# Projecting keys and queries before values in an attention block

## The chip, the cores and the metric

The kernel runs on one NeuronCore of a Trainium2 chip. The metric is the device time of one execution in microseconds, as the median of repeated runs. Five engines work side by side, each in its own order of instructions: PE (matrix products and transposes), DVE (VectorE), ACT (ScalarE), POOL (GpSimd) and SP, which here issues the loads and stores. They wait for each other by semaphores.

## The reference

One layer of a bidirectional encoder block on 512 tokens of 1024 values, all in float32:

```
h    = rms_norm(x) * (1 + scale1) + shift1
proj = h @ w_in        # columns: qa ka va | qb kb vb | gates
# branch A: 12 heads of 64, three groups with (window, dilation) =
#           (128, 1), (512, 4), (2048, 16), merged by their denominators
# branch B: 8 heads, differential attention:
#           (softmax(q1 k1) - lam * softmax(q2 k2)) v, then a sub-norm
# q and k of both branches: rms norm per head, then rotary embedding
mixed = sigmoid(gate_a) * (oa @ w_proj_a) + sigmoid(gate_b) * (ob @ w_proj_b)
x = x + gate1 * (mixed @ w_out)
x = x + gate2 * PEER(rms_norm(x) * (1 + scale2) + shift2)
```

The change lies in the part from `proj` to the two attention branches. The experts' part (PEER), which takes most of the span, comes after it.

## The kernel before

**A projection.** `proj` multiplies the normed input, held as eight transposed tiles, with a chunk of up to 512 columns of `w_in`. For each of the eight slices of the depth, `piece` loads 128 rows of the chunk (tile raw), and splits them into a high part (ScalarE, line 91, whi) and a low part (line 92, wlo, on VectorE or GpSimd); PE then issues three matmuls (lines 86 to 88) for each of four blocks of tokens. The four sums of a chunk fill four PSUM banks (`pmat`, tile pj, four buffers), which are freed when `done` has read them. A 512-column chunk is 96 matmuls.

**Three users of it.** `v_chunk` projects values, and ScalarE copies the sums to va (branch A) or vb (branch B) at line 479. `heads` projects keys or queries: ScalarE copies the sums to four tiles kraw at line 408 (there are eight kraw in all), and then come the head norms and the rotary embedding, on ScalarE (413), VectorE (414, a Newton iteration at 97 to 103, 426 to 428) and GpSimd (421, 429, the last step). `gate` adds a bias on VectorE (line 651) and applies a tanh.

**The units.** `pair_psum` (line 435) transposes the keys or queries of two heads out of the kraw tiles. `dil_units` goes through branch A in two pairs of head slots, eight units each: scores (lines 475, 476, 543, 544, on VectorE 546 to 553) and, two units later, an out (transposes at 561, ScalarE's copies at 563, the products with va at 568, VectorE's 570). `dif_units` goes through branch B in two halves of 16 units: scores at 475 and 476, VectorE 605 to 611, ScalarE 606, and an out (617, 619, products with vb at 623, 625).

**Their order.** The first chunks run alone (`run`). After that `merge` writes units (main) and projections (side) alternately: after each unit, as many slices of the side stream as its estimated cost times a ratio calls for. `seq` strings chunks one after the other, and `with_ada` adds parts of the modulation vectors' loads. The side streams are: beside the first dilated pair, the keys and queries of the second pair (384 columns each); beside the second pair, vb 0 and the keys and queries of the first half of branch B; beside the first half, vb 1 and the keys k1 and queries q1 of the second half (q1 goes to a tile of its own, not to kraw); beside the second half, three gate chunks and the projection of branch A. The fourth gate chunk, the projection of branch B and the rest follow.

**Who decides the order on an engine.** The program's order is a priority only. A list scheduler places the instructions of each engine at build time, by a timeline that it works out itself, as soon as it takes their inputs and buffers for ready. A tile of a rotating pool is had when its earlier user's last reader is done. The order on each engine is then fixed.

Of the kernel before, what the change touches and what calls it, by code (L numbers as in the profile page):

```python
# [45 lines left out]
def merge(main, side, ratio):  # L46

    a = b = 0.0
    live = True
    for c in main:  # L50
        a += c
        while live and b < a * ratio:
            try:
                b += next(side)
            except StopIteration:
                live = False
    if live:
        drain(side)
# [73 lines left out]
def front(K, A):  # L132
# [267 lines left out]
    def heads(c0, n, tab, jp=None, dst=None):  # L400

        H = n // 64
        raws = {}
        ss = wf.tile([128, 4, H], F32, name=f"ss{H}", bufs=2)

        def done(a, ps):
            raws[a] = dst[a] if dst else kq.tile([128, 512], F32, name="kraw", tag="kraw", bufs=8)[:, :n]
            nc.scalar.activation(raws[a], ps, AF.Copy)

        yield from proj(hT, win, c0, n, 8, done, jp)  # L410
        for a in range(4):
            sq = f2()
            nc.scalar.activation(sq[:, :n], raws[a], AF.Square)
            nc.vector.tensor_reduce(out=ss[:, a, :], in_=sq[:, :n].rearrange("p (h i) -> p h i", i=64), op=OP.add, axis=AX)
        v = wf.tile([128, 4 * H], F32, name=f"v{H}", bufs=2)
        nc.vector.tensor_scalar(v, ss.rearrange("p a h -> p (a h)"), 1.0 / 64, EPS, op0=OP.mult, op1=OP.add)
        r = wf.tile([128, 4, H], F32, name=f"r{H}", bufs=2)
        rsqrt(r.rearrange("p a h -> p (a h)"), v, 4 * H)
        for a in range(4):
            raw = raws[a].rearrange("p (h i) -> p h i", i=64)  # L420
            nc.gpsimd.tensor_tensor(raw, raw, r[:, a, :, None].to_broadcast([128, H, 64]), op=OP.mult)
            m2 = f2()
            m2v = m2[:, :n].rearrange("p (h i) -> p h i", i=64)
            C = ropeC[tab][:, a, None, :].to_broadcast([128, H, 64])
            S = ropeS[tab]
            nc.vector.tensor_tensor(m2v[:, :, 0:32], raw[:, :, 32:64], S[:, a, None, 0:32].to_broadcast([128, H, 32]), op=OP.mult)
            nc.vector.tensor_tensor(m2v[:, :, 32:64], raw[:, :, 0:32], S[:, a, None, 32:64].to_broadcast([128, H, 32]), op=OP.mult)
            nc.vector.tensor_tensor(raw, raw, C, op=OP.mult)
            nc.gpsimd.tensor_tensor(raws[a], raws[a], m2[:, :n], op=OP.add)
        return [raws[a] for a in range(4)]  # L430
# [47 lines left out]
    def v_chunk(c0, n, dst):  # L478
        return proj(hT, win, c0, n, 8, lambda a, ps: nc.scalar.activation(dst[:, a, :], ps, AF.Copy))

    def run(g):
        while True:
            try:
                next(g)
            except StopIteration as e:
                return e.value
# [24 lines left out]
    for i in range(2):  # L511
        q = []
# [6 lines left out]
    va = dil.tile([128, 4, 768], F32, name="va")  # L519
# [12 lines left out]
    def dil_keys(jp, ok):  # L532
        return k_pair(pair_psum(ok, 0)), k_raw(pair_psum(ok, 1)), k_raw(pair_psum(ok, 2))

    def dil_queries(oq):
        return q_pair(pair_psum(oq, 0)), q_raw(pair_psum(oq, 1), 0), q_raw(pair_psum(oq, 2), 1)
# [57 lines left out]
    vbs = [vp.tile([128, 4, 512], F32, name=f"vb{i}", tag=f"vb{i}") for i in range(2)]  # L594
# [61 lines left out]
    def seq(*gens):  # L656
        for g in gens:
            yield from g
# [6 lines left out]
    def with_ada(g, vecs=ada2):  # L665
        while True:
            try:
                c = next(g)
            except StopIteration as e:
                return e.value  # L670
            next(vecs, None)
            yield c

    run(v_chunk(1536, 512, va[:, :, 0:512]))
    run(v_chunk(2048, 256, va[:, :, 512:768]))
    ok = run(heads(768, 384, 0, 0))
    oq = run(heads(0, 384, 1, 0))
    late_ = cst.tile([128, 1], F32, name="later")
    nc.vector.tensor_copy(late_, oq[0][:, 0:1])
    mark[0] = late_  # L680
# [2 lines left out]
    def keep(name, g):  # L683
        res[name] = yield from g

    k, q = dil_keys(0, ok), dil_queries(oq)
    merge(pipelined(dil_units(0, k, q)),
          seq(keep('k', heads(768, 384, 0, 1)), keep('q', heads(0, 384, 1, 1))), 3.0)
    k, q = dil_keys(1, res['k']), dil_queries(res['q'])
    merge(pipelined(dil_units(1, k, q)),  # L690
          with_ada(seq(v_chunk(4352, 512, vbs[0]), keep('k', heads(3328, 512, 2)), keep('q', heads(2304, 512, 3)))), 3.0)
    dil.close()
    dif = Pool("dif")
    ob = dif.tile([128, 4, 1024], F32, name="ob")
# [2 lines left out]
    dx = Pool("dx")  # L697
    q1 = gen.tile([128, 4, 512], F32, name="q1", tag="Tl1")
    merge(pipelined(dif_units(0, res['k'], res['q'])),
          with_ada(seq(v_chunk(4864, 512, vbs[1]), keep('k1', heads(3840, 512, 2)),  # L700
                       keep('q1', heads(2816, 512, 3, dst=[q1[:, a, :] for a in range(4)])))), 1.5)
    oaT = ([], [])

    def oa_rows():
# [572 lines left out]
```

## Time and profile before

| | us |
|---|---|
| median of 3 runs | 2019.08 (2017.93 to 2024.71) |
| the profiled execution | 2023.89 |
| its span in the profile | 2022.1 |
| PE busy in the span | 1879.2 |
| DVE busy | 1629.3 |
| ACT busy | 842.7 |
| POOL busy | 819.5 |

Busy times of matmuls overlap and are modelled, so a busy PE is not a PE at its peak. Times in rows are microseconds from the start of the span. In brackets behind an instruction stands the idle time of its engine just before it, and who ended it.

### The profile page before, as it was taken

The numbers are of one execution on the slowest core, as the hardware profiler recorded it, in microseconds if no ns is written. First come the engines' busy times: TensorE is split into PE (matmuls) and PEld (weight loads), VectorE is DVE, ScalarE is ACT, GpSimd is POOL, SyncE is SP. The second block draws the span as 40 slices with busy tenths as digits, with TensorE's granted clock in tenths as the row PEclk, the third lists the DMA queues.
The fourth block names the chain that finished last, engine by engine and source line by source line (L and its number), as shares of the span: only waits on it lengthen the run. The fifth ranks groups of instructions, "written<-read, shape, count | busy, mean of one in ns | idle before, by whom it ended". The sixth has DMA issues, their size and how long they took to land.

```text
span 2022.1 us, 28380 instructions
## 1 busy us (share of the span) xinstructions
PE 1879.2 (93%) x9858; PEld 1623.4 (80%) x9858; DVE 1629.3 (81%) x3228; ACT 842.7 (42%) x1330; POOL 819.5 (41%) x582
## 2 busy tenths in 40 slices
PE   6999998989899899999999999979997999899898
PEld 5987777778677788999989999958885788679676
DVE  7489585886875759999989999579886887888778
ACT  3444454645633333345455566423332333233222
POOL 2554332352145531012533000465565454656445
PEclk9999998999999999999999999989998999899999
DMA  7334242132256322578779867889988988998888
GB/s 260 91 114 121 62 142 62 32 89 84 58 156 211 132 79 66 157 246 284 250 272 319 283 231 254 295 320 363 336 288 302 354 310 312 353 337 323 299 308 292
DMA packets 206418, 447.30 MB, mean 221 GB/s; under 512 B 17298, under 2 KB 104643, under 8 KB 206147
## 3 DMA queue, kind: packets, MB, share of 16 engines
q1 hardware_dynamic: 168592, 309.14, 45.3%
q0 software_dynamic: 36864, 134.23, 18.4%
q10 hardware_dynamic: 818, 2.12, 0.3%
q8 instruction: 77, 1.26, 0.3%
q14 instruction: 67, 0.54, 0.1%
HBM read 397.20 MB, written 48.23 MB: 220 GB/s over the span
## 4 chain that ended last, share of the span: by engine, by line
PE 38%; DVE 13%; issue 11%; DMA 9%; POOL 7%; ACT 1%; SPq 0%; POOLq 0%; DVEq 0%; ACTq 0%
PE y L1220 10%; PE pj L86 8%; PE pj L87 8%; PE pj L88 8%; POOL gat L1058 4%; POOL wlo L92 2%; PE pg L1137 2%; DMA gat<-expert_v,eidx 2%; DVE wlo L92 2%; DMA gat<-expert_u,eidx 2%; DMA am<-gls 2%; DMA raw<-uT 1%; DMA raw<-expert_v 1%; DMA raw<-w_ada 1%; DVE mr L933 1%
## 5 line engine op out<-in xcount | busy, mean ns | idle before, releaser
L91 ACT ACTIVATE whi<-raw 128x1024 fp32r<-128x1024 f32 (+3 forms) x431 | 382.2, 893 | 460.3 <-PE pj L88 116.8
L92 POOL TENSOR_TENSOR wlo<-raw,whi 128x1024 fp32r<-128x1024 f32 (+2 forms) x140 | 275.6, 1972 | 465.2 <-ACT whi L91 437.5
L92 DVE TENSOR_TENSOR wlo<-raw,whi 128x1024 fp32r<-128x1024 f32 (+3 forms) x291 | 326.4, 1126 | 100.0 <-ACT whi L91 99.2
L86 PE MATMUL pj<-h2h,whi 128*128 128x384 f32 x1008 | 345.7, 343 | 6.3 <-ACT am L879 6.3
L88 PE MATMUL pj<-h2h,wlo 128*128 128x384 f32 x1008 | 343.6, 341 | 7.3 <-DVE wlo L92 4.1
L87 PE MATMUL pj<-h2l,whi 128*128 128x384 f32 x1008 | 344.3, 342 | 0.0
L1058 POOL DMA_INDIRECT gat<-expert_u,eidx x128 | 174.3, 1362 | 325.9 <-DVE gscr L1064 152.7
L1220 PE MATMUL y<-wlo,ah 128*128 128x512 f32 x768 | 248.0, 405 | 44.2 <-POOL wlo L92 44.2
L1058 POOL DMA_INDIRECT gat<-expert_v,eidx x128 | 199.4, 1557 | 204.4 <-DVE acc L1076 127.8
L1220 PE MATMUL y<-whi,al 128*128 128x512 f32 x768 | 240.6, 402 | 0.0
L1220 PE MATMUL y<-whi,ah 128*128 128x512 f32 x768 | 229.7, 396 | 7.4 <-ACT ah L91 6.3
L1220 PEld LDWEIGHTS y<-wlo,ah 128*128 128x128 f32 x768 | 147.0, 193 | 83.7 <-POOL wlo L92 48.5
L86 PE MATMUL pj<-whi,hh 128*128 128x512 f32 (+2 forms) x512 | 192.5, 389 | 9.5 <-DVE gA L651 4.4
L91 ACT ACTIVATE ah<-am 128x384 fp32r<-128x384 f32 x128 | 67.0, 524 | 318.7 <-PE y L1220 217.4
L87 PE MATMUL pj<-wlo,hh 128*128 128x512 f32 (+2 forms) x512 | 196.7, 385 | 2.3 <-DVE wlo L92 2.3
L86 PEld LDWEIGHTS pj<-h2h,whi 128*128 128x128 f32 x1008 | 191.2, 190 | 9.0 <-ACT am L879 7.5
L88 PEld LDWEIGHTS pj<-h2h,wlo 128*128 128x128 f32 x1008 | 190.8, 189 | 8.8 <-DVE wlo L92 4.8
L87 PEld LDWEIGHTS pj<-h2l,whi 128*128 128x128 f32 x1008 | 190.9, 189 | 1.2
L88 PE MATMUL pj<-whi,hl 128*128 128x512 f32 (+2 forms) x512 | 191.5, 381 | 0.0
L1076 DVE SCALAR_TENSOR_TENSOR acc<-gat,wts,acc 128x1024 f32<-128x1024 f32 x127 | 182.0, 1433 | 11.5 <-DMA gat<-expert_v,eidx 10.8
L1220 PEld LDWEIGHTS y<-whi,ah 128*128 128x128 f32 x768 | 143.8, 188 | 42.3 <-ACT ah L91 8.1
L1220 PEld LDWEIGHTS y<-whi,al 128*128 128x128 f32 x768 | 147.7, 192 | 36.6 <-DVE al L92 0.2
(313 smaller groups left out, 3274.0 us busy)
## 6 DMA issues: line engine op xcount, KB each, us to landing
raw<-uT SPq DMA_DIRECT2D x128, 512.0 KB
raw<-expert_v SPq DMA_DIRECT2D x128, 512.0 KB
gd<-stage SPq DMA_DIRECT2D x48, 512.0 KB
gch<-gd SPq DMA_DIRECT2D x16, 1536.0 KB
raw<-w_in SPq DMA_DIRECT2D x88, 256.0 KB
am<-gls SPq DMA_DIRECT2D x96, 192.0 KB
gls<-am SPq DMA_DIRECT2D x94, 192.0 KB
raw<-w_ada SPq DMA_DIRECT2D x64, 256.0 KB
```

The lines of the kernel that those rows point to most:

```text
L86: nc.tensor.matmul(ps, lh, rh, start=start, stop=False)
L87: nc.tensor.matmul(ps, lh, rl, start=False, stop=False)
L88: nc.tensor.matmul(ps, ll, rh, start=False, stop=stop)
L91: nc.scalar.activation(hi, raw, AF.Copy)
L92: (eng or nc.vector).tensor_tensor(lo, raw, hi.bitcast(F32), op=OP.subtract)
L933: nc.vector.match_replace(out=r, in_to_replace=v[:, 0:8], in_values=s, imm_value=-3.0e38)
L1058: nc.gpsimd.indirect_dma_start(out=t, out_offset=None, in_=src, in_offset=bass.IndirectOffsetOnAxis(ap=eidx[:, s:s + 1], axis=0))
L1076: nc.vector.scalar_tensor_tensor(acc, t, wts[:, s:s + 1], acc, op0=OP.mult, op1=OP.add)
L1137: nc.tensor.matmul(p[:, j * 128:j * 128 + 128], oh[1][:, :, q + j], pcs[i][:, q + j, :], start=i == 0, stop=i == 1)
L1220: nc.tensor.matmul(ys[b][n], l[:, bs], r[:, n * 512:n * 512 + 512], start=n_ == 0 and i == 0, stop=n_ == 127 and i == 2)
```

## The change

Three chunks of values move behind the keys and queries that stand beside them. Nothing else is changed.

```
     run(v_chunk(1536, 512, va[:, :, 0:512]))
-    run(v_chunk(2048, 256, va[:, :, 512:768]))
     ok = run(heads(768, 384, 0, 0))
     oq = run(heads(0, 384, 1, 0))
+    run(v_chunk(2048, 256, va[:, :, 512:768]))
...
     merge(pipelined(dil_units(1, k, q)),
-          with_ada(seq(v_chunk(4352, 512, vbs[0]), keep('k', heads(3328, 512, 2)), keep('q', heads(2304, 512, 3)))), 3.0)
+          with_ada(seq(keep('k', heads(3328, 512, 2)), keep('q', heads(2304, 512, 3)), v_chunk(4352, 512, vbs[0]))), 3.0)
...
     merge(pipelined(dif_units(0, res['k'], res['q'])),
-          with_ada(seq(v_chunk(4864, 512, vbs[1]), keep('k1', heads(3840, 512, 2)),
-                       keep('q1', heads(2816, 512, 3, dst=[q1[:, a, :] for a in range(4)])))), 1.5)
+          with_ada(seq(keep('k1', heads(3840, 512, 2)),
+                       keep('q1', heads(2816, 512, 3, dst=[q1[:, a, :] for a in range(4)])),
+                       v_chunk(4864, 512, vbs[1]))), 1.5)
```

## Rows read from the trace of the kernel before

**Rows 1.** The page: busy time by engine, and the chain that ended last.

```profile
PE 1879.2 (93%) x9858; PEld 1623.4 (80%) x9858; DVE 1629.3 (81%) x3228; ACT 842.7 (42%) x1330; POOL 819.5 (41%) x582
...
PE 38%; DVE 13%; issue 11%; DMA 9%; POOL 7%; ACT 1%; SPq 0%; POOLq 0%; DVEq 0%; ACTq 0%
```

**Rows 2.** Timeline of ACT: the copies that end a projection (start, duration, instruction).

```profile
63.31 2.04 ACT L479 ACTIVATE va<-pj 128x512 f32<-128x512 f32 x4
...
74.22 1.31 ACT L479 ACTIVATE va<-pj 128x256 f32<-128x256 f32 x4
...
90.22 1.01 ACT L408 ACTIVATE kraw<-pj 128x384 f32<-128x384 f32 x2
...
106.86 1.01 ACT L408 ACTIVATE kraw<-pj 128x384 f32<-128x384 f32 x2
...
195.59 0.58 ACT L479 ACTIVATE vb<-pj 128x512 f32<-128x512 f32 x1
...
229.04 1.58 ACT L408 ACTIVATE kraw<-pj 128x512 f32<-128x512 f32 x3
...
369.86 1.57 ACT L408 ACTIVATE kraw<-pj 128x512 f32<-128x512 f32 x3
```

**Rows 3.** Timeline of PE: transposes of keys and queries; first and last matmul of gate chunks.

```profile
109.22 0.44 PE L435 MATMUL pt<-ident,kraw 128*128 128x128 f32 x2 [0.61 <-POOL kraw L429]
111.23 0.69 PE L435 MATMUL pt<-ident,kraw 128*128 128x128 f32 x2 [1.57 <-POOL kraw L429]
...
226.02 2.54 PE L435 MATMUL pt<-ident,kraw 128*128 128x128 f32 x16
...
368.73 0.60 PE L435 MATMUL pt<-ident,kraw 128*128 128x128 f32 x4
...
439.54 0.79 PE L86 MATMUL pj<-whi,hh 128*128 128x512 f32 x1 [4.42 <-DVE gA L651]
...
503.11 0.39 PE L88 MATMUL pj<-whi,hl 128*128 128x512 f32 x1
```

**Rows 4.** Timeline of POOL: the last rope step of the first queries.

```profile
131.71 1.55 POOL L429 TENSOR_TENSOR kraw<-kraw,f 128x384 f32<-128x384 f32 x1 [0.50 <-DVE g L183]
```

**Rows 5.** Windows: stretch, length, busy by engine (instructions), clock, DMA share, GB/s.

```profile
75.00:91.00 16.00, 16.00 (x94) 16.00 (x94) 2.28 (x4) 5.32 (x12) 4.22 (x7) 1.00 0.38 110
...
108.00:116.00 8.00, 5.82 (x28) 5.27 (x27) 7.65 (x21) 3.64 (x8) 4.95 (x4) 0.79 0.27 79
116.00:144.00 28.00, 25.22 (x141) 24.33 (x140) 22.86 (x45) 15.26 (x29) 16.23 (x16) 0.94 0.40 119
...
158.00:195.00 37.00, 34.87 (x186) 28.09 (x186) 35.72 (x76) 14.37 (x31) 18.72 (x16) 1.00 0.40 116
195.00:229.00 34.00, 32.55 (x180) 26.89 (x180) 10.12 (x18) 14.70 (x29) 6.14 (x5) 1.00 0.36 108
...
340.00:368.00 28.00, 21.81 (x121) 16.06 (x120) 24.69 (x50) 20.46 (x50) 2.31 (x3) 0.94 0.04 10
...
404.00:440.00 36.00, 29.24 (x149) 24.01 (x148) 33.93 (x63) 14.77 (x33) 21.89 (x16) 0.98 0.21 57
```

**Rows 6.** Windows for line 568 alone: PE, PEld, clock, DMA share, GB/s.

```profile
195.00:229.00 34.00, 6.25 (x48) 6.44 (x48) 1.00 0.36 108
```

**Rows 7.** Timeline of PE: two outs of dilated units with little projection between.

```profile
258.43 1.55 PE L568 MATMUL pt<-va,eT 128*128 128x64 f32 x12
...
262.37 1.00 PE L568 MATMUL pt<-va,eT 128*128 128x64 f32 x8
```

**Rows 8.** Windows for line 623 alone; a differential unit has eight records.

```profile
404.00:440.00 36.00, 4.21 (x32) 4.19 (x32) 0.98 0.21 57
...
456.00:503.00 47.00, 4.21 (x32) 4.18 (x32) 1.00 0.26 80
503.00:536.00 33.00, 11.32 (x80) 9.76 (x80) 1.00 0.16 47
```

## Prediction before the change was measured

> **What bounds the kernel now.** I read the page first. PE is busy for 93% of the span, yet its share of the chain that ended last is 38%, with 13% DVE and 11% in which nothing visible is waited for [rows 1]. So a busy PE is no proof of a bound, and the stretch that the edit touches has to be read by itself. I took it in four steps: ScalarE's copies that end each projection (they date the chunks), PE's timeline around the transposes that read keys and queries, GpSimd's last rope step, and last the busy times by stage.
>
> The copies give the order and the pace [rows 2]: the 256-column value chunk takes 74.22 − 63.31 = 10.9 us of PE, the first keys follow at 90.22, the first queries at 106.86, the first vb at 195.59, the next keys at 229.04, k1 at 369.86. Two different limits show by stage [rows 5]. From 116 to 195 us DVE is nearly full (22.86 of 28 us, 35.72 of 37): the rope of keys and queries and the score sums of the first dilated pair. From 195 to 229 it is the other way: PE 32.55 of 34 us, DVE 10.12. From 340 to 368 PE runs differential units alone (21.81 of 28).
>
> The third thing to see is a buffer. Keys and queries share eight kraw tiles, four per call of heads(). The key copies at 229.04 come right behind the sixteen transposes at 226.02 that free four of them, and the k1 copies at 369.86 right behind the transposes at 368.73 [rows 2, 3]. Until such a copy is made, its chunk holds all four pj banks and no other projection can start.
>
> **The change, part by part.** Nothing is removed or added. The same loads, splits, matmuls and copies are issued; three chunks of values move behind the keys and queries beside them, with the weight loads on SP's queue and their splits on ScalarE and DVE.
>
> First move: the 256-column chunk goes behind the first queries. Keys and queries come forward by its 10.9 us. The rope that follows is long: the queries' copies begin at 106.86 and GpSimd's last sum ends at 131.71 + 1.55 = 133.3 [rows 2, 4], 26 us, and the first scores wait for it. DVE can take that work earlier, since it is busy for only 2.28 of 16 us from 75 to 91 [rows 5]. In PE's order the moved chunk now lies where PE waits 0.61 and 1.57 us for the keys' rope [rows 3] at a granted clock of 0.79 [rows 5], so those 2.2 us of PE should go too. How far the first dilated units come forward isn't shown by any row: at least the 2.2 us of PE, at most 10.9. The bounds are far apart; DVE's 13.7 idle us from 75 to 91 decide for the upper end, and I take 10.
>
> Second move: the 512 columns of keys take the slot that vb 0 has, so their matmuls end at about 195.6 − 10 = 186 instead of just before 229. But their copies need the four kraw tiles that the second dilated pair's keys hold until their transposes, which stand behind all outs of the first pair. Behind the waiting copies are queued the four pj banks, so PE has no projection, and the queries, vb 0 and all later chunks wait. That is a new stall. What is left to do in it: four outs. With projections between them four outs took the 34 us from 195 to 229 (48 records of line 568, 12 to a unit [rows 6]), 8.5 us each, while DVE stood idle: they wait their turn in PE's order. With little projection about, two outs stood 262.37 − 258.43 = 3.9 us apart [rows 7]. So the stall is 4 × 3.9 = 16 us, the transposes and the first key copy take some 2.5 more, as now from 226.02 to 229.04, and the copies come at 186 + 16 + 2.5 = 204.5. Call the lead X = 229 − 204.5 = 24.5 us. Bounds: X is 2 if only the 2.2 us above are won and the outs keep their pace, and 30 if the outs run ahead of the keys and only half of the stall is left. I take 24.5, because DVE has no work left in that stretch that could slow an out.
>
> The lead has a price: at the key copies, PE has done the keys but not vb 0, so one chunk less. From here on the chunks follow as before with other names (queries, vb 0, k1, q1, vb 1 where queries, vb 1, k1, q1, gate 0 stood), so the wait of k1 for kraw, 340 to 368, stays as long as it is and moves by X. Third move, vb 1 behind q1: k1 and q1 keep their places, vb 1 takes that of gate 0. In both orders a vb is projected before the units that read it start.
>
> One difference: gate 0's results leave the banks through DVE, and there PE waited 4.42 us for them behind the rope of q1 [rows 3]; from 404 to 440 PE is busy for only 29.24 of 36 us [rows 5]. The copies of vb are ScalarE's, which is busy 14.77 us there. I count the 4.4 us as won; the bounds are 0 and 6.8, the whole idle.
>
> The owed chunk is paid at the end, when the gates are projected beside the second half of the differential units. Two gate chunks take 503.1 − 439.5 = 63.6 us there [rows 3], 31.8 each. Meanwhile units go on: four in the 47 us from 456, against ten in the 33 us from 503 without projections [rows 8]; so about four units are done in the added 31.8 us, if, as from 404 to 440, a chunk carries four [rows 8], and 4 × 3.3 = 13.2 us of the bare stretch at the end go away. Net price 18.6 us.
>
> Sum: 24.5 (lead) − 31.8 + 13.2 + 4.4 = 10.3 us faster. Everything behind 548 us follows the gates and the last units in order and moves with them. The profiled execution took 2023.9 us (span 2022.1 and 1.8 around it), 4.8 over the median of the runs; so 2013.6 for such an execution and 2019.1 − 10.3 = 2008.8 for the median. I predict 2009.
>
> A rule that speaks against the change stands in the Trainium skill, page Perfetto Trace Analysis, section Optimization Strategy: a gap that keeps returning on the engine that should be saturated can mean that there is no buffer for the next tile. Here the trace agrees: both waits for kraw sit where a chunk of keys ends. By that rule alone the keys' earlier start would be worth nothing, which is the second rival below.
>
> **The rivals.** No measurable change (within 6 us, 0.3% of the time, about what the measurement can tell): the lead shrinks to 8 to 20 us, because DVE, full from 116 to 195, takes the earlier rope only partly, and the planner, which doesn't follow program order, fits the chunks otherwise. At X = 14 the sum is −31.8 + 13.2 + 4.4 + 14 = 0. For it: DVE's shares [rows 5]. Against it: the idle DVE before 91 us. That the planner undoes the moves belongs here as well; the four banks speak against it, as they bind a chunk to its order.
>
> Slower: the kraw wait in the first dilated pair. The keys end early, find no tile, and the outs keep their pace of 8.5 us, as the planner may still hold them back for work that it expects on other engines. Then the copies come at 229 − 2 at best and the owed chunk is paid in full: 2 − 31.8 + 13.2 + 4.4 = 12 us slower, about 2031, or 16 without the relief at gate 0. It decides as soon as the first 512-wide key copy comes later than 221 us (X under 8). For it: the copy at 229.04 is bound to the transposes already, and so is that at 369.86 [rows 2, 3]. Against it: without projections PE has nothing else to put between the outs.
>
> **How the numbers follow.** Forecast 0.48, no change 0.28, slower 0.24. The forecast's own range, X from 20 to 30, is 2003 to 2013. For 8 in 10 I leave out the far ends: a lead of 30 with all 6.8 us won at gate 0 and some luck beyond, 1998 (0.1 below it), and the upper part of the slower case, 2030 (0.1 above it). Faster by over 0.3% 0.48, within 0.28, slower 0.24.
>
> **What would show it.** Right: first kraw copies near 79 and 96 us, the first scores (line 475) some 10 us earlier than now, no idle of PE at the keys' first transposes; four 512-wide kraw copies near 205, ahead of the first vb copy, and before them a stretch of some 16 us with outs and no projection; k1's copies near 345 with as long a wait as now; the last gate chunk beside the units ending near 508 and four units fewer behind it. Wrong: scores that don't come forward, outs 8 us apart in the stall, key copies after 221, or a stall of k1 that grows, since I left it alone.

## The result, and the profile after

The changed kernel takes 2040.95 us in the median of six runs (2031.21 to 2051.0); the kernel before, run beside it, 2019.06 (2017.93 to 2024.71). The ratio is 1.0097, with a 95% interval from 1.0071 to 1.0122: slower by about 1%, 20 us. The forecast of 2009 was wrong in its sign.

The page of the changed kernel's profiled execution (2031.21 us, span 2029.4), to be set against [rows 1]; the first line is busy time by engine, the second the chain that ended last:

```profile
PE 1888.5 (93%) x9858; PEld 1631.3 (80%) x9858; DVE 1631.6 (80%) x3228; ACT 846.6 (42%) x1330; POOL 814.8 (40%) x582
...
PE 55%; DVE 22%; DMA 9%; issue 7%; POOL 4%; ACT 3%; SPq 0%; DVEq 0%; ACTq 0%; POOLq 0%
```

The same number of instructions on every engine; PE's busy time rose by 9.3 us. This execution was the fastest of the six. Its experts' part, whose code the change doesn't touch, ran shorter than in the kernel before, so the two are best compared ahead of it: the first DVE instruction of the experts' part (line 931 before, 932 after) starts at 716.1 us before and at 737.0 after. Those 20.9 us are the change.

The timeline of ACT in the changed kernel, the copies that end a projection, answers to [rows 2]:

```profile
78.34 1.01 ACT L408 ACTIVATE kraw<-pj 128x384 f32<-128x384 f32 x2
...
94.98 1.01 ACT L408 ACTIVATE kraw<-pj 128x384 f32<-128x384 f32 x2
...
110.40 1.26 ACT L479 ACTIVATE va<-pj 128x256 f32<-128x256 f32 x4
...
217.21 1.57 ACT L408 ACTIVATE kraw<-pj 128x512 f32<-128x512 f32 x3
...
292.11 1.56 ACT L479 ACTIVATE vb<-pj 128x512 f32<-128x512 f32 x3
...
359.77 2.06 ACT L408 ACTIVATE kraw<-pj 128x512 f32<-128x512 f32 x4
```

The first keys and queries came at 78 and 95, as forecast. The 512-wide keys came at 217.21 where 204.5 was forecast: a lead X of 11.8 us, not 24.5. k1 came at 359.77 (forecast 345), and its wait for kraw grew, where the forecast had it as long as before. The timelines of PE, of the kernel before and below it of the changed one, show the last matmul of k1's chunk and the next matmul of a projection:

```profile
339.72 0.39 PE L88 MATMUL pj<-whi,hl 128*128 128x512 f32 x1
...
370.58 0.43 PE L86 MATMUL pj<-whi,hh 128*128 128x512 f32 x1
```

```profile
318.54 0.40 PE L88 MATMUL pj<-whi,hl 128*128 128x512 f32 x1
...
360.50 0.42 PE L86 MATMUL pj<-whi,hh 128*128 128x512 f32 x1
```

From the one to the other it is 30.9 us before and 42.0 us in the changed kernel. In both, the copies are made right behind the transposes that free the tiles (those at 358.64 here, of which the copies follow at 359.77), so k1's chunk came 21.2 us earlier, its copies only 10.1.

The timeline of PE in the changed kernel, first the keys' transposes and the first scores, then the stretch of the stall (idle time and its releaser in brackets):

```profile
99.06 0.44 PE L435 MATMUL pt<-ident,kraw 128*128 128x128 f32 x2 [1.56 <-POOL kraw L429]
...
129.82 0.39 PE L475 MATMUL ps<-pairs 128*128 128x512 f32 x1
...
197.58 0.39 PE L88 MATMUL pj<-whi,hl 128*128 128x512 f32 x1
201.70 0.69 PE L561 MATMUL pt<-ident,s 128*128 128x128 f32 x2 [3.73 <-DVE oa L570]
202.18 2.66 PE L568 MATMUL pt<-va,eT 128*128 128x64 f32 x12
204.63 1.49 PE L561 MATMUL pt<-ident,s 128*128 128x128 f32 x6
206.44 2.82 PE L568 MATMUL pt<-va,eT 128*128 128x64 f32 x12 [0.32 <-ACT eT L563]
209.05 1.49 PE L561 MATMUL pt<-ident,s 128*128 128x128 f32 x6
210.86 2.82 PE L568 MATMUL pt<-va,eT 128*128 128x64 f32 x12 [0.32 <-ACT eT L563]
213.47 3.78 PE L435 MATMUL pt<-ident,kraw 128*128 128x128 f32 x16
217.86 0.79 PE L86 MATMUL pj<-whi,hh 128*128 128x512 f32 x1 [0.61 <-ACT kraw L408]
```

The first scores come at 129.8; in the kernel before they came at 144.3. The keys' wait for the rope [rows 3] is still there, 1.56 us. The key matmuls end at 197.58. Then PE has no projection for 20.3 us, and the sixteen transposes take 3.78 us where they took 2.54 [rows 3]. The timeline of DVE in the changed kernel shows what PE's 3.73 us stand for:

```profile
197.06 0.75 DVE L205 SCALAR_TENSOR_TENSOR acc<-raw,sil,acc 128x512 f32<-128x512 f32 x1 [1.93 <-DMA raw<-w_ada]
197.73 0.95 DVE L549 TENSOR_REDUCE sm<-s 128x1 f32<-128x768 f32 x1
200.63 0.75 DVE L205 SCALAR_TENSOR_TENSOR acc<-raw,sil,acc 128x512 f32<-128x512 f32 x1 [1.96 <-DMA raw<-w_ada]
...
201.38 0.27 DVE L570 TENSOR_SCALAR oa<-pt,sm 128x64 f32<-128x64 f32 x1
```

DVE is nearly idle there but not free. Two accumulations of a modulation row (line 205) wait for their loads, 1.93 and 1.96 us, and behind both in DVE's order stands line 570, which reads the sums of an earlier out and so frees the buffer that PE waits for.

Windows of the changed kernel by stage, answering to [rows 5] (stretch, length, busy time by engine and instructions, granted clock, DMA share, GB/s):

```profile
199.00:217.00 18.00, 14.66 (x66) 13.28 (x66) 4.31 (x10) 6.01 (x13) 0.34 (x1) 0.56 0.28 85
195.00:229.00 34.00, 29.02 (x129) 24.51 (x128) 14.14 (x32) 16.08 (x31) 4.26 (x4) 0.70 0.22 68
324.00:360.00 36.00, 27.68 (x145) 19.79 (x143) 30.77 (x59) 25.67 (x62) 4.08 (x6) 0.86 0.00 1
404.00:440.00 36.00, 34.70 (x179) 28.32 (x178) 26.50 (x50) 17.40 (x40) 16.71 (x14) 1.00 0.30 91
464.00:517.00 53.00, 53.00 (x267) 44.12 (x266) 34.45 (x65) 31.39 (x69) 12.53 (x11) 1.00 0.31 85
```

From 195 to 229 PE has 129 matmul records where it had 180, at a granted clock of 0.70, where it was 1.00. In the stall itself the mean clock is 0.56, near the lower of its two levels, 1.2 GHz. From 404 to 440, PE is fuller than before (34.70 against 29.24 us). Windows for line 623 alone answer to [rows 8]:

```profile
404.00:440.00 36.00, 5.26 (x40) 5.23 (x40) 1.00 0.30 91
464.00:517.00 53.00, 5.26 (x40) 5.23 (x40) 1.00 0.31 85
517.00:550.00 33.00, 9.97 (x72) 8.83 (x72) 1.00 0.14 40
```

Beside the last two gate chunks, five units (40 records) are done where four had been done beside two [rows 8]; behind them, nine in 33 us where there had been ten. The last gate of this stretch ends its matmuls some 12 us later than before (its sums leave the banks at 516.25, before from 503.91 on).

### The profile page after: what moved, and what is told of

The parts are those of the page before. It is cut to its first block, busy times and chain, and to the rows that moved or that the text cites. A ratio compares the mean times of both kernels' runs of the same rounds, so it can differ in the third digit from the quotient of the medians.

```text
span 2029.4 us, 28375 instructions
## 1 busy us (share of the span) xinstructions
PE 1888.5 (93%) x9858; PEld 1631.3 (80%) x9858; DVE 1631.6 (80%) x3228; ACT 846.6 (42%) x1330; POOL 814.8 (40%) x582
## 4 chain that ended last, share of the span: by engine, by line
PE 55%; DVE 22%; DMA 9%; issue 7%; POOL 4%; ACT 3%; SPq 0%; DVEq 0%; ACTq 0%; POOLq 0%
PE y L1221 17%; PE pj L86 10%; PE pj L87 10%; PE pj L88 10%; DVE wlo L92 3%; DMA raw<-w_ada 2%; PE pg L1138 2%; DMA raw<-expert_v 2%; DMA gat<-expert_v,eidx 2%; POOL gat L1059 2%; DMA am<-gls 1%; POOL wlo L92 1%; DVE f L427 1%; DMA raw<-uT 1%; DVE mr L934 1%
## 5 line engine op out<-in xcount | busy, mean ns | idle before, releaser
L92 POOL TENSOR_TENSOR wlo<-raw,whi 128x1024 fp32r<-128x1024 f32 (+3 forms) x140 | 268.3, 1920 | 487.3 <-ACT whi L91 446.6
L1059 POOL DMA_INDIRECT gat<-expert_v,eidx x128 | 203.9, 1593 | 204.8 <-DVE acc L1077 134.4
L86 PE MATMUL pj<-whi,hh 128*128 128x512 f32 (+2 forms) x512 | 193.6, 387 | 10.7 <-ACT q L408 4.4
L1077 DVE SCALAR_TENSOR_TENSOR acc<-gat,wts,acc 128x1024 f32<-128x1024 f32 x127 | 190.7, 1502 | 10.6 <-DMA gat<-expert_v,eidx 9.9
L91 ACT ACTIVATE ah<-am 128x384 fp32r<-128x384 f32 x128 | 67.1, 525 | 293.1 <-PE y L1221 221.5
L1065 DVE SCALAR_TENSOR_TENSOR gscr<-gat,h2tok 128x1024 bf16<-128x1024 f32 x128 | 166.9, 1304 | 8.4 <-DMA gat<-expert_u,eidx 7.8
```

Of the source, the lines that this page charges most:

```text
L86: nc.tensor.matmul(ps, lh, rh, start=start, stop=False)
L91: nc.scalar.activation(hi, raw, AF.Copy)
L92: (eng or nc.vector).tensor_tensor(lo, raw, hi.bitcast(F32), op=OP.subtract)
L1059: nc.gpsimd.indirect_dma_start(out=t, out_offset=None, in_=src, in_offset=bass.IndirectOffsetOnAxis(ap=eidx[:, s:s + 1], axis=0))
L1065: nc.vector.scalar_tensor_tensor(scr, t, 1.0, h2tok, op0=OP.mult, op1=OP.mult, accum_out=act[:, s:s + 1])
L1077: nc.vector.scalar_tensor_tensor(acc, t, wts[:, s:s + 1], acc, op0=OP.mult, op1=OP.add)
```

## The experiments

All of them are set against the kernel before, run in the same job. Since a few us matter and the experts' part scatters by more (26 runs of the kernel before in one job spread from 2007.5 to 2032.0), each run is also read at three points of its trace: the last product of branch A (line 717 before, "branch A"), the last split behind the transposes of the mixed rows (line 771, on DVE, "mixed"), and the first DVE instruction of the experts' part ("experts"). Each of these readings is of one execution; the kernel before and h4, which changes next to nothing, differ by 0.2, 0.8 and 1.8 us. The last five columns are worked out from PE's timeline: the work that PE has done from 60 us to the time given, less that of the kernel before. Each matmul counts as what it takes back to back at full clock (0.2345 us for 512 columns, 0.1735 for 384, 0.117 for 256, 0.11 for 128 or less); g1 and g2 have 15 us less of it to do. The versions that leave this part as it is (f1, and h4 nearly) agree with the kernel before within 1 us.

| run | us | ratio (95%) | branch A | mixed | experts | work at 220 | 380 | 440 | 500 | 560 |
|---|---|---|---|---|---|---|---|---|---|---|
| before | 2019.06 | 1 | 553.7 | 639.1 | 716.1 | 0 | 0 | 0 | 0 | 0 |
| changed | 2040.95 | 1.0097 (1.0071 to 1.0122) | 563.4 | 656.5 | 737.0 | -15.5 | -14.3 | -15.9 | -13.5 | -13.4 |
| e1 | 2030.71 | 1.0050 (1.0028 to 1.0073) | 559.2 | 644.4 | 725.1 | -2.9 | -3.6 | 0.0 | -3.4 | -5.4 |
| e2 | 2025.60 | 1.0014 (0.9996 to 1.0032) | 549.7 | 643.1 | 720.3 | -11.8 | -2.3 | 0.1 | 1.2 | 0.5 |
| e3 | 2031.32 | 1.0047 (1.0030 to 1.0064) | 553.4 | 645.9 | 723.6 | 0.8 | -7.7 | -5.6 | -3.0 | -2.8 |
| e4 | 2038.36 | 1.0077 (1.0053 to 1.0102) | 567.8 | 655.2 | 735.6 | -8.2 | 1.7 | 0.8 | -10.4 | -15.9 |
| f1 | 2060.33 | 1.0194 (1.0177 to 1.0211) | 550.5 | 677.9 | 758.3 | -0.2 | -0.5 | -0.9 | -0.5 | -0.5 |
| f2 | 2074.63 | 1.0255 (1.0227 to 1.0284) | 565.5 | 691.8 | 772.2 | -17.1 | -18.5 | -20.2 | -17.7 | -14.1 |
| f3 | 2051.76 | 1.0158 (1.0141 to 1.0175) | 548.2 | 640.9 | 741.5 | 0.0 | 0.1 | -0.7 | 1.4 | 2.6 |
| f4 | 2075.62 | 1.0246 (1.0200 to 1.0293) | 562.2 | 656.4 | 759.6 | -16.7 | -15.4 | -17.5 | -15.1 | -11.5 |
| g1 | 2016.31 | one run | 540.7 | 633.4 | 713.9 | -4.3 | -8.8 | -7.4 | -7.7 | -5.4 |
| g2 | 2031.69 | one run | 552.5 | 645.2 | 725.8 | -16.7 | -16.2 | -19.0 | -16.4 | -17.4 |
| g3 | 2031.67 | 1.0046 (1.0031 to 1.0062) | 577.0 | 643.9 | 721.3 | 0.2 | 2.7 | 0.6 | 2.8 | -0.2 |
| g4 | 2043.81 | 1.0104 (1.0063 to 1.0144) | 592.0 | 657.4 | 737.7 | -17.2 | -16.9 | -19.1 | -16.5 | -8.7 |
| h1 | 2035.95 | 1.0065 (1.0040 to 1.0090) | 559.4 | 653.7 | 734.4 | 0.7 | 10.7 | 17.1 | -2.3 | -8.0 |
| h2 | 2033.58 | 1.0051 (1.0032 to 1.0069) | 562.0 | 650.8 | 728.3 | -17.2 | -2.2 | 2.2 | -1.8 | -9.8 |
| h3 | 2029.05 | 1.0035 (1.0012 to 1.0058) | 558.4 | 647.0 | 727.2 | -9.1 | 0.8 | 2.4 | -0.4 | -6.3 |
| h4 | 2022.29 | 1.0002 (0.9980 to 1.0024) | 553.5 | 639.9 | 717.9 | 0.0 | 0.7 | 0.5 | 0.5 | 0.5 |
| i1 | 2044.42 | 1.0117 (1.0094 to 1.0141) | 561.9 | 652.4 | 738.7 | -13.4 | -11.5 | -12.8 | -10.2 | -10.3 |
| i2 | 2027.35 | 1.0029 (1.0011 to 1.0048) | 550.9 | 636.9 | 719.9 | 0.6 | 0.3 | -0.7 | 1.9 | 1.0 |

**e1 to e3: each move alone.** Each is the kernel before with one of the three hunks of the change: e1 the 256-column chunk, e2 vb 0, e3 vb 1.

> Only the 256-column value chunk goes behind the first queries; the other two value chunks stay first. Stall theory (the loss comes from keys that find no kraw tile in the second move): this part alone brings the first scores from 144 to about 131 us and costs nothing: 2010 to 2020. Debt theory (a value chunk put off is paid for at the end beside the last units): the 256-column chunk is put off by two chunks only, so nothing either, 2015 to 2023. Planner theory (any edit reshuffles later stages and the time moves by 10 us or more without a local cause): anything between 2005 and 2045, with the shift arising behind the attention stage.

> Only vb 0 goes behind the keys and queries beside the second dilated pair. Stall theory: this carries the loss, since the keys' copies wait for the kraw tiles; PE without projection for 15 us or more ahead of the first 512-wide kraw copy, last out of the differential units (line 623) 10 to 20 us later than the 545 of before, time 2028 to 2042. Debt theory: the same stall is seen, but it is repaid by the earlier queries, and the last out moves by less than 5 us: 2017 to 2024. Planner theory: as for the first part, no pattern.

> Only vb 1 goes behind k1 and q1. Stall theory: k1 meets the kraw wait one chunk earlier (its matmuls end near 311 instead of 340, the tiles come free at 368 or somewhat earlier because the units then run alone for longer), so some 5 to 12 us of loss here too: 2022 to 2032. Debt theory: vb 1 takes the slot of the first gate chunk and one gate chunk more is left beside the last units; the last out moves by +8 to +15 us from 545: 2027 to 2035. Planner theory: no pattern.

e1 loses 0.50%, e2 0.14%, e3 0.47%; their sum, 1.11%, is near the whole change's 0.97%, but the parts don't add up: at branch A the three stand 5.5 us later, 4.0 earlier and 0.3 earlier, the whole change 9.7 later. In e3 all of the 7.5 us at experts come behind branch A, in e2 8.2 us do. e2, which has the stall, is the only one level with the kernel before: 11.8 us behind in work at 220, and level from 440 on. Neither the stall nor the debt theory had a loss for e1, and 5.5 of its 9.0 us at experts arise ahead of the end of branch A, so not behind the stage as the planner theory has it; its cause stays open. The timelines of ACT in e1 and, below it, in e2, at the first 512-wide keys:

```profile
231.39 1.57 ACT L408 ACTIVATE kraw<-pj 128x512 f32<-128x512 f32 x3
```

```profile
214.39 1.58 ACT L408 ACTIVATE kraw<-pj 128x512 f32<-128x512 f32 x3
```

With the first move alone the keys come 2.3 us later than at 229.04 [rows 2], although the first scores came at 131.5. With the second alone they come at 214.39.

**e4: the changed kernel with other tiles for the first 512-wide keys.** The 512-wide keys are copied into vb 1's tiles, which are free at that time.

```
-          with_ada(seq(keep('k', heads(3328, 512, 2)), keep('q', heads(2304, 512, 3)), v_chunk(4352, 512, vbs[0]))), 3.0)
+          with_ada(seq(keep('k', heads(3328, 512, 2, dst=[vbs[1][:, a, :] for a in range(4)])),
+                   keep('q', heads(2304, 512, 3)), v_chunk(4352, 512, vbs[0]))), 3.0)
```

> The changed kernel, with the keys of the first half of branch B copied to the tile that later holds vb 1 (free until then) instead of four kraw tiles. Neither these keys nor k1 then have to wait for kraw. Stall theory: the copies come when the matmuls end, near 200 instead of 217 us, the PE gap before them and the bare units at 324 to 360 are filled, and the last out of the differential units comes 15 us or more before the 556 of the changed kernel: 2015 to 2025, at or under the kernel before. Debt theory: the gaps are filled, but the units are pushed back by the same amount, last out 550 to 558, time 2033 to 2045. Planner theory: no pattern.

The keys' copies now come at 202.2, and the time is not better beyond the uncertainty (1.0077 against 1.0097). PE's work is 1.7 us ahead of that of the kernel before at 380 and 15.9 us behind at 560. But the borrowed tiles bring a wait of their own, as the timeline of PE in e4 shows (last matmul of vb 1's chunk, last transposes of the keys, next projection):

```profile
374.66 0.40 PE L88 MATMUL pj<-whi,hl 128*128 128x512 f32 x1
...
393.60 0.60 PE L435 MATMUL pt<-ident,vb 128*128 128x128 f32 x4
...
395.32 0.48 PE L86 MATMUL pj<-whi,hh 128*128 128x512 f32 x1
```

vb 1's sums wait until the keys have left its tiles, 20.7 us without a projection. So e4 is no test of a kernel without the wait. That the stall by itself is the loss is refuted by e2, which has it and loses nothing clear of noise; e4 adds only that these tiles don't help.

**f1, f2: the order behind the attention stage held fixed.** In both kernels the instructions of PE, DVE, ACT and POOL from the fourth gate chunk to mixed_rows(1) are taken in program order, so both have the same order there.

```
+    pin = K.tc.manual_schedule(engines={mybir.EngineType.PE, mybir.EngineType.DVE, mybir.EngineType.Activation, mybir.EngineType.Pool})
+    pin.__enter__()
     drain(with_ada(gate(1536, br, [gB[1][:, a] for a in range(4)]), ada3))
...
     mixed_rows(1)
+    pin.__exit__(None, None, None)
```

> The kernel before, with PE, DVE, ACT and POOL held to program order from the fourth gate chunk to the last transposes of the mixed rows, so that the planner can't place that part differently. It is the reference for its pair. Each theory: 2019 to 2040, the pinned part (from the last sum of branch A, line 717, to the last split at line 771) some 85 to 100 us long instead of 85.

> The changed kernel with the same part held to program order. Rearrangement theory (the changed kernel loses 8 us behind the attention stage only because the planner orders the branch stage otherwise): the pinned part is as long here as in its reference, within 2 us, and the lag in the trace at line 771 is that of the last sum of branch A, about 10 us. Rival (the later start itself costs more, through loads or buffers that the attention stage hands on): the pinned part is again 7 us longer or more.

Both are slower for it, by more than was expected, but the part from branch A to mixed now takes 127.4 us in f1 and 126.3 in f2, the same. Without the fixed order it takes 85.4 us before and 93.1 after. So 7.7 us of the change's loss lie behind the stage, in the order that the planner chose there, and go when the order is the same. What is left between f1 and f2, 15.0 us at branch A and 13.9 at experts, is the stage's own (9.7 us at branch A where the order is free).

**f3, f4: the fourth gate chunk beside the units, written last.** In both kernels `gate(1536, ...)` moves to the end of the side stream, behind branch_a(1), and its results go to kraw tiles.

```
-                       oa_rows(), branch_a(0), branch_a(1))), 1.5)
+                       oa_rows(), branch_a(0), branch_a(1),
+                       gate(1536, kq, gB1))), 1.5)
...
-    drain(with_ada(gate(1536, br, [gB[1][:, a] for a in range(4)]), ada3))
```

> The kernel before, with the fourth gate chunk moved into the side stream beside the last differential units, behind the projection of branch A, where these units run with little projection; its result goes to kraw tiles. Bare-stretch theory (the attention stage loses its time where units run without projections): its 20 us of PE work fill a stretch where PE waits, and the last split of the mixed rows (639 before) comes 8 to 14 us earlier, time 2007 to 2016. Rival (DVE is what the last units wait for): the chunk only lengthens them, 639 plus or minus 4, time 2015 to 2025.

> The changed kernel with the same fourth gate chunk beside the last units. Bare-stretch theory: it gains as much as its counterpart, 8 to 14 us, and the two still differ by about 10 us: 2020 to 2032. Rival (the order of keys and values is what fails to fill the tail): it gains much more than its counterpart and comes within 4 us of it.

These told nothing of the units: the chunk still ran behind them (its last sums at 571.8 in f3), and the steps of the modulation rows that used to run beside it were left over, so that mixed to experts grew to 100.6 us from 77.0.

**g1, g2: less PE work.** In both kernels the third of three products (low part of the input, high part of the weight) is left out for the two 512-column chunks of vb: 64 matmuls, 15 us of PE.

```
...
-    nc.tensor.matmul(ps, lh, rl, start=False, stop=False)
-    nc.tensor.matmul(ps, ll, rh, start=False, stop=stop)
+    nc.tensor.matmul(ps, lh, rl, start=False, stop=stop and K.light)
+    if not K.light:
+        nc.tensor.matmul(ps, ll, rh, start=False, stop=stop)
...
+                K.light = wv is win and c0 in (4352, 4864)
...
```

> The kernel before, with the third of the three products of each 128x128 block (low part of the input by high part of the weight) left out for the two 512-column chunks of vb alone: 64 matmuls of 512 columns fewer, some 64 x 0.2345 = 15 us of PE work; copies, splits and loads stay as they are. PE's total sets the attention stage: the last out of the second half (line 717, 553.7 in the kernel before) comes 10 to 15 us earlier, and the end of the span with it. The order of keys and buffers sets it: the chunks are only shorter in places where PE waits anyway, and line 717 moves by less than 5 us.

> The changed kernel with the same 64 matmuls of the vb chunks left out (low part of the input by high part of the weight, the two 512-column chunks of vb alone). PE's total: line 717, 563.4 in the changed kernel, comes 10 to 15 us earlier, so that the distance to the run beside it (the kernel before with the same left out) stays near 10 us. If the loss were tied to the vb chunks that now stand late, it would shrink to less than half of that.

The last product of branch A in the timelines of DVE: of the kernel before, of g1, of the changed kernel, of g2.

```profile
553.68 0.68 DVE L717 SCALAR_TENSOR_TENSOR gA<-gA,pj 128x512 f32<-128x512 f32 x1
```

```profile
540.74 0.68 DVE L722 SCALAR_TENSOR_TENSOR gA<-gA,pj 128x512 f32<-128x512 f32 x1
```

```profile
563.36 0.68 DVE L718 SCALAR_TENSOR_TENSOR gA<-gA,pj 128x512 f32<-128x512 f32 x1
```

```profile
552.54 0.68 DVE L723 SCALAR_TENSOR_TENSOR gA<-gA,pj 128x512 f32<-128x512 f32 x1
```

Of 15 us of work taken out, 12.9 come back at the end of the stage in g1 and 10.8 in g2, with copies, loads and splits as they were, and the distance between the two stays (11.8). So PE's work makes most of the stage's length, and what PE idles the rest. Each is one run.

**g3, g4: the fourth gate chunk beside the units, ahead of branch A.** As f3 and f4, but the chunk stands ahead of oa_rows(), and branch_b(0) takes two modulation steps at a time.

```
+                       gate(1536, kq, gB1),
                        oa_rows(), branch_a(0), branch_a(1))), 1.5)
...
-    drain(with_ada(branch_b(0), ada3))
+    drain(with_ada(with_ada(branch_b(0), ada3), ada3))
```

> The kernel before, with the fourth gate chunk taken into the stream beside the second half's units (its results go to kraw tiles) and the branch's other steps behind it. Bare stretches: between the units' end and the chunk alone behind them, PE ran 10 to 12 units bare at 3.3 us; a chunk of some 31 us projected beside units takes four units along, so the last gate matmul comes 8 to 13 us earlier than 577.8 and the time is 2007 to 2013. PE's total alone: the work is the same and only its order changes; the gate's end stays within 3 us, the time within 0.3% of the kernel before.

> The changed kernel with the same move of the fourth gate chunk. Bare stretches: the changed kernel has a bare tail of 10 units as well, so it gains 8 to 13 us too and stands some 15 to 20 us over the run beside it. If the loss of the change were the bare tail alone, this run would come within 5 us of the run beside it.

This time the chunk did run beside units (its last sums at 534.3 in g3). Windows of the kernel before, and below it of g3:

```profile
503.00:545.00 42.00, 34.21 (x218) 27.34 (x216) 34.43 (x68) 31.22 (x74) 4.96 (x5) 1.00 0.15 43
545.00:580.00 35.00, 33.13 (x153) 26.65 (x152) 29.94 (x69) 10.63 (x20) 16.75 (x18) 1.00 0.51 151
```

```profile
503.00:545.00 42.00, 38.86 (x214) 31.86 (x212) 28.82 (x52) 25.16 (x57) 11.21 (x10) 1.00 0.33 100
545.00:580.00 35.00, 24.36 (x117) 18.26 (x116) 25.11 (x71) 11.90 (x25) 6.38 (x11) 0.95 0.21 61
```

PE's first column gains 4.65 us in the bare tail and loses 8.77 right behind it, where the chunk used to cover the last units' chains. Slower by 0.46% in the kernel before; the gain that both were expected to have isn't there.

**h1 to h4: k1's wait taken away.** k1 is copied into the tiles of gA[1], which are free until their gate; for that the gates 512 and 1024 change places. h1 is the kernel before with this, h2 the changed kernel, h3 is e4 with it (neither wait for kraw is left), h4 the kernel before with the gates' places changed and nothing else. The cut shows parts of lines.

```
...
-keep('k1', heads(3840, 512, 2))
+keep('k1', heads(3840, 512, 2, dst=gA[1]))
...
-gate(0, dif, gA[0]), gate(512, dif, gA[1]), gate(1024, vp, [gB[0][:, a] for a in range(4)]),
+gate(0, dif, gA[0]), gate(1024, vp, [gB[0][:, a] for a in range(4)]), gate(512, dif, gA[1]),
```

> The kernel before with k1 written to the tiles of gA[1], which are free until the gate that is projected last, so that k1's copies wait for no kraw tile (the gates 512 and 1024 change places for it). The waits for kraw set the time: PE's bare stretch from 340 to 368 goes, PE's work is some 7 us ahead at 380 and stays so, time 2010 to 2014. Work is only moved: 7 us ahead at 380, but the gates end as much earlier and more units run bare behind them; time within 6 us of the kernel before, line 717 within 3 us of 553.7.

> The changed kernel with k1 in the tiles of gA[1] in the same way; the first 512-column keys wait for kraw as in the changed kernel. The waits set the time: some 10 us less than the changed kernel, 2030, line 717 near 553. Work is only moved: within 6 us of the changed kernel, line 717 near 563.

> The changed kernel with both waits for kraw away: the first 512-column keys in vb 1's tiles (as in e4) and k1 in those of gA[1]. The waits set the time: PE's lost time up to 380 falls below that of the kernel before, and the run comes to within 3 us of h1, 2010 to 2014. Work is only moved: PE's work leads by 7 us or more at 380 and is behind again at 560; time 2035 or more, as e4.

> The kernel before with the gates 512 and 1024 in the other order and nothing else, the control for h1 to h3. Both theories: within 0.3% of the kernel before.

h4 moves nothing. In the changed order the ratios fall as waits go: 1.0097, then 1.0077 without the first (e4, within the uncertainty), 1.0051 without the second (h2), 1.0035 without both (h3). In the kernel before the same step makes it worse: h1 stands at 1.0065. Windows of h1, and below them the row of PE in which its lead ends:

```profile
320.00:380.00 60.00, 60.00 (x298) 49.07 (x298) 37.70 (x62) 35.99 (x74) 15.99 (x15) 1.00 0.24 67
380.00:440.00 60.00, 58.90 (x310) 49.30 (x308) 43.75 (x85) 33.36 (x72) 21.51 (x18) 1.00 0.23 66
440.00:520.00 80.00, 61.63 (x304) 47.88 (x303) 65.46 (x125) 47.87 (x105) 26.58 (x25) 0.89 0.21 63
```

```profile
460.93 0.50 PE L86 MATMUL pj<-whi,hh 128*128 128x512 f32 x1 [4.42 <-DVE gB L651]
```

PE is full up to 440 and 17.1 us ahead of the kernel before. Then gate 1024, early too, holds the four banks until its result tile, which has vb 0's place, is free behind the first half's last unit (456.1) and DVE is done with the rope that stands ahead of it (460.2); the units of that half run alone, the clock has a mean of 0.89 from 440 to 520, and the lead becomes a lag of 8.0 us by 560. Neither theory as it was written had that: the lead was not only given back.

A third chunk waits as well: gate 512, now the last of the three, for the tiles that k1 borrowed. In h1 its last matmul, k1's last transposes, and the first DVE instruction that reads its sums:

```profile
486.99 0.39 PE L88 MATMUL pj<-whi,hl 128*128 128x512 f32 x1
...
515.10 0.60 PE L435 MATMUL pt<-ident,gA 128*128 128x128 f32 x4
```

```profile
515.41 2.48 DVE L651 TENSOR_TENSOR gA<-pj,bg 128x512 f32<-128x512 f32 x4 [0.50 <-PE pt L435]
```

h2 and h3 have the same (from 490.5 and 488.3 on, the sums are read at 517.6 and 514.8), and h3 also e4's wait of vb 1, 10.7 us there. So none of these versions is one without waits; each puts the wait for kraw off to the next user of the tiles it takes.

**i1, i2: the mixed rows between the branches.** In the runs so far that leave this part's code alone, branch A to experts takes 170 us or more where the first transpose of the mixed rows comes 11 us or more after the last product of branch_b(0), and 162 to 169 where it comes within 4 us. Here both kernels have mixed_rows(0) written between the two branches.

```
     drain(with_ada(branch_b(0), ada3))
+    mixed_rows(0)
     drain(with_ada(branch_b(1), ada3))
-    mixed_rows(0)
     mixed_rows(1)
```

> The changed kernel with mixed_rows(0) written between branch_b(0) and branch_b(1). If the late transposes cost the changed kernel its time behind the stage: the last transpose of the mixed rows (line 771) comes within 89 us of the last product of branch_a (line 717), instead of 93.1, 717 to 931 takes 162 to 169 us instead of 173.6, and the time falls by 5 to 9 us to some 2032 to 2036. If the order only goes along: 717 to 931 stays at 170 or more and the time within 0.2% of the changed kernel.

> The kernel before with mixed_rows(0) between the two branches. Where the late transposes are the cost, the kernel before, which has them early by itself, gains little: 717 to 931 stays at 160 to 165 us, the time within 0.2%, and i1 stands 10 to 15 us over it, which is the attention stage's part alone.

i1 has the transposes early and yet takes 176.8 us from branch A to experts (738.7 - 561.9); i2 takes 169.0, 6.6 more than the kernel before. So the place of these transposes is not what costs the changed kernel its time there. i1 and i2 are 11.0 us apart at branch A.

No version that does all of the work ran faster than the kernel before; e2 and h4 are level with it.

## Why the prediction was wrong

The forecast sum was 10.3 us faster; the traces have 20.9 us slower at the experts' start. The 31.2 us between are 12.7 + 11.1 + 11.2, less 3.8 that came back on the way, in which two smaller terms, k1's wait and the relief at gate 0, are contained.

**The lead X, 12.7 us short: the main error.** "Their matmuls end at about 195.6 - 10 = 186" took the units' lead for the projections' lead. The units did come forward by 14.5 us, more than the 10 taken. But the key matmuls stand in PE's order behind the same work as before, merely sorted otherwise, and PE is nearly full there [rows 5]. Such a set ends earlier only by the idle time that leaves it. The forecast named 2.2 us of that, and they did not go: PE's idle time from 60 to 200 us was 15.6 us before and 19.4 after. The set ended at 197.58, and e1 shows the first move alone: no lead, 231.39. The stall, its place and its four tiles were right. Its length was so in part by luck: 16 + 2.5 = 18.5 us from the keys' end to their copies were taken, from four outs. The changed kernel has 19.6, from three slower outs, a wait of PE and slow transposes, and e2, with four outs, has 22.6 (191.8 to 214.39). With X = 11.8 and the other terms as they stood, the sum would have been 2.4 us slower, the rival of no change.

**"DVE has no work left in that stretch that could slow an out"** was wrong by mechanism, small in size: it had little work, but waits for loads stood in its order, and behind two of them PE waited 3.73 us. Outs stood 4.3 and 4.4 us apart (202.18, 206.44, 210.86), not the 3.9 taken, and the transposes ran at the lower clock level. The rival of the slow outs (8.5 us apart) did not happen, though its sign, slower, did.

**"The wait of k1 for kraw ... stays as long as it is and moves by X"** failed: it grew by 11.1 us, which the prediction itself had named as a sign of being wrong. k1's chunk moves with the projections, the transposes that free its tiles move with the units, and the projections had gained more. PE's idle time from 320 to 380 us went from 11.0 to 16.9 us. e3, with the third move alone, has this wait too (43.5 us), e2 has not (28.9).

**The relief at gate 0 (4.4 us)** came, but little was won: PE's wait of 4.42 us there is gone, one of 4.37 us for the copies of q1 stands in the changed kernel at 392.02, and the idle time from 380 to 460 us fell by 0.7 us.

**The owed chunk and the bare tail, 11.1 us short.** By the last gate, 3.8 us of the missing lead had come back: the changed kernel is 11.75 us late there (506.97 to 518.72, the ends of the gate's last sums) where 31.8 - 24.5 - 4.4 = 2.9 was forecast. But "four units fewer" behind it did not come: branch A is 9.7 us late, so the tail gave back 2.1 us and not 13.2. The owed chunk did not lie beside added units of the second half. It lay beside the first half: gate 0's sums end at 458.3 before the second half's first scores at 464.91, which were late themselves (456.64 before). From 464 to 517 five units are done, one more than the four of [rows 8]. PE is busy for all of the 53 us from 464 to 517; where it is that full, a chunk put beside units takes their place and does not take them along. g1 and g2 show the same from the other side.

**"Everything behind 548 us follows ... and moves with them", 11.2 us short.** Branch A to experts grew from 162.4 to 173.6 us, with the same work. f1 and f2 show that this goes when the order there is held the same (207.8 and 206.7 us). That the mixed transposes alone make it is excluded by i1; which other part of the order does is open. In part it is the luck of the kernel before: of the eleven other versions that have this part's code unchanged and its order free (changed, e1 to e4, g1, g2, h1 to h4), none is as quick there, and their median is 170.2 us.

**What the stage itself lost, by stretch.** PE's idle time from 60 to 560 us (time less work as in the table) is 63.2 us before and 76.6 after. By stretch, before and after: 60 to 200, 15.6 and 19.4; 200 to 260, 8.5 and 13.1; 260 to 320, 7.6 and 7.5; 320 to 380, 11.0 and 16.9; 380 to 460, 10.1 and 9.4; 460 to 560, 10.6 and 10.4. So 10.5 of the 13.4 us lie in the two stretches in which keys wait for kraw, and 3.8 ahead of them. That is where the time went; that these waits are the cause is not shown by taking them away, since e4 and h1 to h3 put other waits in their place. They had the work forward at 380 or 440 (e4 by 1.7, h1 by 17.1, h3 by 2.4 us) and lost it later. A version with tiles that nothing else needs was not run. Why h3 lags less than e4 is answered in part by the trace: vb 1 waits 10.7 us in it, not 20.7. Why e2 makes up for the stall by 380 and the changed kernel doesn't shows in k1's wait: behind the stall both catch up until 320 (e2 from 11.8 to 3.8 us, the changed kernel from 15.5 to 8.4), then e2 waits for 28.9 us, as the kernel before does, and the changed kernel for 42.0 and is 14.3 us behind at 380. This is read from the traces; no run has the second and the third move without the first.

The rule of the Trainium skill that the prediction weighed (Perfetto Trace Analysis, Optimization Strategy: a gap that keeps returning can mean a missing buffer) holds here for what the gap is: with other tiles for the keys (h3) it goes, and PE is busy for 31.67 us from 195 to 229 and 59.67 from 320 to 380, with the change as it stands for 29.02 and 51.17. In time, these tiles were worth 0.62% for both in the changed order (h3 against the changed kernel) and minus 0.65% for k1's in the order before (h1). They were borrowed from later chunks, so this is not the worth of tiles of their own.

## What to carry to other kernels

On an engine that is nearly full, sorting its work anew brings the end of the whole set forward only by the idle time that disappears: count idle, not how much earlier one stream starts. If two streams cover each other's waits, a chunk that is taken forward is missing as cover later; ask which stretch loses it before a lead is counted as a gain. A tile that is borrowed to end one wait can start another: ask who writes it next, and when. And under a list scheduler "everything behind moves along" is a term of the sum with a price of its own: here a third to a half of the loss was in code that the change didn't touch.

## What the runs showed of the hardware that was not expected

An engine that looks idle in a window can still be the one that is waited for: DVE was busy for 4.31 of 18 us from 199 to 217, and yet PE waited 3.73 us for it, since two instructions ahead of the one that PE needed waited for loads (1.93 and 1.96 us).

PE's granted clock has a mean of 0.56 in that stretch: it stands at 0.50, the lower level, from 201.2 to 221.5 us. PE had been without a matmul from 198.0 to 201.7, had transposes and small products alone after that, and projections again from 217.86. Sixteen transposes of the same form took 3.78 us there and 2.54 in the kernel before.

The same DVE instruction takes 0.41 or 1.51 us, and the slow ones lie beside POOL's work; the timelines of DVE and, below, of POOL in the changed kernel:

```profile
239.03 0.41 DVE L427 TENSOR_TENSOR f<-kraw,ropeS 128x256 f32<-128x256 f32 x1
...
240.30 1.51 DVE L427 TENSOR_TENSOR f<-kraw,ropeS 128x256 f32<-128x256 f32 x1
```

```profile
237.10 1.72 POOL L92 TENSOR_TENSOR wlo<-raw,whi 128x512 fp32r<-128x512 f32 x1
240.12 1.41 POOL L429 TENSOR_TENSOR kraw<-kraw,f 128x512 f32<-128x512 f32 x1 [1.29 <-DVE kraw L428]
```

The quick one lies in POOL's gap from 238.8 to 240.1, the slow one beside POOL's addition. Of the 32 instructions of this form (lines 426 and 427) in the changed kernel, 13 took 0.41 or 0.42 us, seven of them with POOL idle, and 19 took 0.66 to 1.52, all of them beside POOL's work.
